# The embedding gate of an encoder layer as seven block products instead of eight, on the sums of h that the FFN needs anyway

## The chip, the cores and the metric

The kernel runs on one core of a Trainium2 chip, written in Bass with the Tile framework. Tile inserts the waits; on an engine that the code has not put under "manual schedule" it also chooses the order of the instructions, and on the others they stand as the code issues them. Each engine runs its own list in order, and an instruction that waits holds up all that stand behind it on that engine. The metric is the device time of one execution in microseconds (us). A profile of one execution goes with it, with the start and length of each instruction.

## The reference

One layer of a bidirectional encoder, 1024 tokens by 1024 features in float32. What matters here comes after the attention:

```python
h   = layer_norm(ALPHA * x + mix, ln1)                   # mix = heads @ w_out
g   = h @ w_ffn_gate ;  up = h @ w_ffn_up                # 1024 x 2816 each
ffn = (silu(g) * up) @ w_ffn_down
ple      = p @ w_ple_proj                                # p: 1024 x 256, the per-layer embedding
ple_gate = sigmoid(h @ w_ple_gate)                       # 1024 x 1024, the embedding gate
out = layer_norm(ALPHA * h + ffn + ple_gate * ple, ln2)
```

## The kernel before

Every float32 operand is held as two parts, `hi` (rounded, written by ScalarE's copy) and `lo` (the rest, written by VectorE's subtract): the helper `split`, lines 72 to 74. A product of 128 rows by 512 columns is three matmuls, hi·hi, hi·lo and lo·hi (`mm3`, lines 76 to 79, and `mm3c`, 824 to 828). The first of the three reads only the `hi` parts; the second reads the `lo` of the weights, the third the `lo` of the activations.

The program has these stages: the input projection with retention and attention (up to about 373 us in the profile), the output projection with the first layer norm (to 468 us), the embedding (to 586 us), the FFN's gate and up products, called G (to about 1000 us), and the down product with the second layer norm, called D.

In the output projection, tokens are handled in eight tiles of 128. Tile t's projection is taken out of PSUM by `zpart` (line 629, one half of the features at a time), normalised by `ln1_apply` (641 to 645; between its two halves GpSimd computes the reciprocal square root, line 639), turned by `to_hT` (653 to 663: eight TensorE transposes, ScalarE writes hi, VectorE lo) into the blocks `HB[i, j]`, with i the half of the features and j the half of the tokens, and scaled by ALPHA in place in its accumulator `accs[t]`.

The embedding stage is four calls of `ple(h, half, ...)` (734 to 760), one for each half of the output columns and of the tokens. A call is two parts. First the gate: 8 feature tiles by 4 token tiles by 3 matmuls, in four PSUM banks, so 96 matmuls, and 384 in all. Then four embeddings, each a small product of p's tile with `w_pe` (6 matmuls, lines 752 to 756); sigmoid on ScalarE (758), and on VectorE the product with the embedding (759) and the addition to the accumulator (760). The tile of p is split into a buffer `pt` of which there is one (line 750, tag "p", the 1), so the next tile of p can only be split when the six matmuls on the last one are over. No engine is under manual schedule in this stage, and Tile is free to put other matmuls between the embeddings.

G works with 2 by 2 blocks and seven products in place of eight (Winograd's form of Strassen's scheme). Its sums of the blocks of h, `TT[1]` to `TT[4]`, are made in this stage by VectorE and split (`t_sums`, 766 to 810), spread over the calls of `ple`. G's sums of weights are made by GpSimd (`s_sums`, 859 to 867). All engines are under manual schedule from G on.

Weights come through `unit2` (102 to 111): one DMA of 512 KB into one of two buffers "raw", then two splits. Buffers of TensorE's weights turn over too: eight in all, "w" and "u". PSUM has eight banks of 128 by 512, two with each of the tags mm, s, t, o.

Of the kernel before, what the change touches and what calls it, by code (L numbers as in the profile page):

```python
# [40 lines left out]
def layer(tc, xT, xn, w_first, w_mt, w_rv, w_out, w_pg, w_pe, pT, w_gu, w_dn,  # L41
# [627 lines left out]
    for kt in range(4):  # L669
        if kt % 2 == 0:  # L670
            wbig = ct([P, 2, 2, 2, HF], ("h2", "h3")[kt // 2], dt=F32R)
# [56 lines left out]
    def load_pg(h):  # L728
        r = []
        for k in range(4):  # L730
            r += unit2(w_pg[h, k], *((wp, "w") if k % 2 == 0 else (cpool, "u")))
        return r

    def ple(h, half, wpg, side=()):

        sl = slice(h * HF, (h + 1) * HF)
        bg = [bank(("mm", "s")[k // 2]) for k in range(4)]
        for kt in range(KT):
            hh = HB[kt // 4, half]
            for k in range(4):  # L740
                tt = slice(k * P, (k + 1) * P)
                mm3(bg[k], hh[:, 0, kt % 4, tt], hh[:, 1, kt % 4, tt], wpg[kt][:, 0, :], wpg[kt][:, 1, :],
                    kt == 0, kt == KT - 1)
            if kt % 2 and kt // 2 < len(side):
                side[kt // 2]()
        for k in range(4):
            t = 4 * half + k
            r = ct([P, 2 * P], "pr", 2)
            sp.dma_start(r, pT[t])
            pt = ct([P, 2, 2 * P], "p", 1, F32R)  # L750
            split(r, pt[:, 0, :], pt[:, 1, :])
            b2 = bank("to"[k % 2])
            for q in range(2):
                c = slice(q * P, (q + 1) * P)
                mm3(b2, pt[:, 0, c], pt[:, 1, c], wpe[:, h, 0, q * HF:(q + 1) * HF], wpe[:, h, 1, q * HF:(q + 1) * HF],
                    q == 0, q == 1)
            sg = ct([P, HF], "sg", 2)
            act.activation(sg, bg[k], AF.Sigmoid)
            dve.tensor_tensor(sg, sg, b2, ALU.mult)
            dve.tensor_tensor(accs[t][:, sl], accs[t][:, sl], sg, ALU.add)  # L760

    TT, tails = {}, []

    def t_sums():
# [3 lines left out]
        hi = lambda i, j, c: HB[i, j][:, 0, c, :].bitcast(F32)  # L770
        lo = lambda i, j, c: HB[i, j][:, 1, c, :].bitcast(F32)
        hold = {}

        def both(x, left, right, c):

            dve.tensor_tensor(x, hi(*left, c), hi(*right, c), ALU.subtract)
# [52 lines left out]

# [527 lines left out]
```

## Time and profile before

| | us |
|---|---|
| median of 3 runs | 1233.03 (1231.03 to 1233.54) |
| profiled execution, span from first to last instruction | 1230.3 |
| embedding stage in the profile, first gate matmul to last embedding matmul | 468.20 to 586.27 |
| TensorE busy / VectorE / ScalarE / GpSimd | 1210.4 / 721.4 / 474.9 / 367.4 |

The profile gives no separate time for its execution; the span stands 2.7 us under the median, the part of a run that lies outside the first and the last instruction and the spread of runs together. Times inside the profile are counted from the span's start. A group's busy time can include overlap: a 128 by 512 matmul is shown with 0.39 us, but the next one starts 0.23 us after it. In a row of a timeline, the bracket tells how long the engine had been idle before the instruction and which instruction let it go on.

### The profile page before, as it was taken

To read this page: it belongs to the slowest core of one execution; us is meant where nothing else is said; L and a number is where in the kernel's file an instruction comes from. 1 tells how busy PE (TensorE), PEld (TensorE's weight loads), DVE (VectorE), ACT (ScalarE), POOL (GpSimd) and SP (SyncE) were. 2 spreads that over 40 slices of the span, in tenths; PEclk is the share of its full clock that TensorE was granted. 3 is DMA by queue.
4 is the path that set the end of the run, shared out by engine and by line. 5 is a ranking of instruction groups with operands and counts; after the bars stand their busy time and mean duration, and the time that the engine had idled before them with its cause. 6 is when DMAs were issued, how large, how long until landed. Compare 5 with 4: busy or idle time off the path is not lost.

```text
span 1230.3 us, 16375 instructions
## 1 busy us (share of the span) xinstructions
PE 1210.4 (98%) x5987; PEld 1000.5 (81%) x5987; DVE 721.4 (59%) x1288; ACT 474.9 (39%) x890; POOL 367.4 (30%) x342
## 2 busy tenths in 40 slices
PE   9999999999999999999999999999999999999986
PEld 7888888888888888877888888888888888888874
DVE  5542566666755585883755554455554466773766
ACT  5643124344665024432333323233333325552562
POOL 2000011111010020000774665655646341133241
PEclk9999999999999999999999999999999999999997
DMA  6310010101004313132333222332223169999956
GB/s 253 94 35 1 18 35 19 35 19 35 18 24 161 103 52 103 34 105 111 116 128 129 77 77 103 129 129 78 92 87 129 69 216 327 355 248 222 274 111 190
DMA packets 56689, 139.64 MB, mean 114 GB/s; under 512 B 6816, under 2 KB 8992, under 8 KB 56608
## 3 DMA queue, kind: packets, MB, share of 16 engines
q1 hardware_dynamic: 47968, 121.81, 28.3%
q0 software_dynamic: 8640, 16.78, 7.8%
q8 instruction: 47, 0.77, 0.3%
q14 instruction: 34, 0.28, 0.1%
HBM read 104.75 MB, written 28.57 MB: 108 GB/s over the span
## 4 chain that ended last, share of the span: by engine, by line
PE 91%; DVE 4%; issue 1%; ACT 1%; POOL 1%; DMA 1%; DVEq 0%; SPq 0%; ACTq 0%; POOLq 0%
PE bmm L77 7%; PE bmm L78 7%; PE bmm L79 7%; PE bmm L826 4%; PE bmm L827 4%; PE bmm L828 4%; PE bs L826 4%; PE bs L827 4%; PE bs L828 4%; PE bo L827 4%; PE bo L826 4%; PE bo L828 4%; PE bt L826 4%; PE bt L828 4%; PE bt L827 4%; PE bs L79 2%
## 5 line engine op out<-in xcount | busy, mean ns | idle before, releaser
L77 PE MATMUL bmm<-H,w 128*128 128x512 f32 x240 | 100.7, 419 | 1.1 <-DVE rkq L218 0.9
L79 PE MATMUL bmm<-H,w 128*128 128x512 f32 x240 | 94.4, 393 | 0.0
L78 PE MATMUL bmm<-H,w 128*128 128x512 f32 x240 | 94.1, 392 | 0.0
L74 DVE TENSOR_TENSOR w<-raw,w 128x512 fp32r<-128x512 f32 x80 | 60.3, 763 | 52.6 <-ACT w L73 52.3
L863 POOL TENSOR_TENSOR H<-ln 128x512 f32<-128x512 f32 x22 | 28.4, 1292 | 192.3 <-PE bo L79 111.5
L893 POOL TENSOR_TENSOR ev<-ev 128x512 f32<-128x512 f32 x33 | 54.9, 1664 | 91.4 <-DVE ev L908 38.6
L481 POOL COPY sc<-skb 128x1 f32<-128x1 f32 x64 | 17.8, 288 | 202.7 <-PE bt L502 154.2
L74 DVE TENSOR_TENSOR w<-H,w 128x512 fp32r<-128x512 f32 x44 | 40.6, 924 | 63.9 <-ACT w L73 63.9
L73 ACT ACTIVATE w<-raw 128x512 fp32r<-128x512 f32 x80 | 48.9, 624 | 60.8 <-PE bmm L79 29.6
L897 POOL TENSOR_TENSOR ev<-ev,ev 128x512 f32<-128x512 f32 x44 | 62.7, 1437 | 2.6
L891 ACT ACTIVATE ev<-ev 128x512 f32<-128x512 f32 x33 | 20.9, 633 | 102.3 <-DVE ev L908 102.3
L74 DVE TENSOR_TENSOR u<-H,u 128x512 fp32r<-128x512 f32 x47 | 36.1, 767 | 40.1 <-ACT u L73 39.7
L490 ACT ACTIVATE sc<-sc,st 128x385 f32<-128x385 f32 (+1 forms) x64 | 37.2, 583 | 46.2 <-DVE st L488 46.1
L77 PEld LDWEIGHTS bmm<-H,w 128*128 128x128 f32 x240 | 45.3, 189 | 11.4 <-DVE rkq L218 2.2
L486 DVE CUSTOM_DVE_ANT_0 sc<-cst,bs,skb 128x384 f32<-128x384 f32 (+1 forms) x64 | 35.0, 574 | 32.6 <-PE bs L485 32.6
L79 PEld LDWEIGHTS bmm<-H,w 128*128 128x128 f32 x240 | 45.0, 188 | 10.1
L78 PEld LDWEIGHTS bmm<-H,w 128*128 128x128 f32 x240 | 45.3, 189 | 6.1
L73 ACT ACTIVATE u<-H 128x512 fp32r<-128x512 f32 x47 | 29.6, 631 | 43.1 <-PE bs L828 14.0
L639 POOL TENSOR_TENSOR stt<-stt,cst 128x1 f32<-128x1 f32 x8 | 11.6, 1454 | 99.6 <-DVE stt L638 99.6
L867 POOL TENSOR_TENSOR H<-raw,H 128x512 f32<-128x512 f32 x22 | 37.8, 1717 | 0.0
L448 POOL TENSOR_TENSOR sm<-sm,cst 128x8 f32<-128x8 f32 x8 | 13.9, 1737 | 78.4 <-DVE sm L447 78.4
L73 ACT ACTIVATE w<-H 128x512 fp32r<-128x512 f32 x44 | 27.4, 622 | 24.4 <-PE bs L828 6.3
(644 smaller groups left out, 3719.7 us busy)
## 6 DMA issues: line engine op xcount, KB each, us to landing
ad<-ev SPq DMA_DIRECT2D x33, 512.0 KB, 2.6
raw<-in_w_gu SPq DMA_DIRECT2D x22, 512.0 KB, 4.3
ln<-in_w_gu SPq DMA_DIRECT2D x22, 512.0 KB, 3.5
raw<-ad SPq DMA_DIRECT2D x40, 256.0 KB, 5.8
ln<-ad SPq DMA_DIRECT2D x37, 256.0 KB, 6.4
H<-in_w_dn SPq DMA_DIRECT2D x33, 256.0 KB, 6.8
raw<-in_w_mt SPq DMA_DIRECT2D x14, 512.0 KB, 3.5
h0b<-in_w_dn POOLq DMA_DIRECT2D x24, 256.0 KB, 7.0
```

The source lines that it names most:

```text
L73: act.activation(hi, raw, AF.Copy)
L74: dve.tensor_tensor(lo, raw, hi.bitcast(F32), ALU.subtract)
L77: pe.matmul(o, lh, rh, start=start, stop=False)
L78: pe.matmul(o, lh, rl, start=False, stop=False)
L79: pe.matmul(o, ll, rh, start=False, stop=stop)
L490: act.activation(sc[g][:, :nk + 1], sc[g][:, :nk + 1], AF.Exp, bias=st_[:, 1, j, g:g + 1], accum_out=st_[:, 2, j, g:g + 1])
L826: pe.matmul(o, lh, rh, start=start, stop=False, skip_group_check=True)
L827: pe.matmul(o, lh, rl, start=False, stop=False, skip_group_check=True)
L828: pe.matmul(o, ll, rh, start=False, stop=stop, skip_group_check=True)
L867: pool.tensor_tensor(s[3], a(0, 1), s[0], ALU.subtract)
L893: pool.tensor_tensor(c[:, 1, :], c[:, 0, :], c[:, 1, :], ALU.mult)
L897: pool.tensor_tensor(self.ev[dst][:, 0, :], left, right, op)
```

## The change

The gate `h @ w_ple_gate` is computed in G's form: seven block products `prod(p, ...)` of 48 matmuls each, 336 in all, on `HB` and the same sums `TT`. With it goes:

- The sums of blocks of the gate's weights (products 5, 6, 7 and 3) are made in DRAM. SP issues four DRAM-to-DRAM copies of 1 MB (`wsum_copy`), GpSimd's queue seven DRAM-to-DRAM accumulating DMAs of 1 MB (`wsum_add`), both in the code of the retention stage. SP's and GpSimd's lists are not under manual schedule there.
- The halves of the tokens change places in G and D (`HB` in other buffers, `RIGHT`, `tile_of`), since the sum `TT[3]` is now made from the first half alone, at the stage's start: three VectorE operations of 128 by 1024 on one half of it, three GpSimd operations on the other. `TT[2]`, `TT[1]`, `TT[4]` follow one by one with two VectorE operations for each half.
- VectorE combines the seven products out of PSUM into tiles `u`, `v`, `f` (128 by 512): 24 operations in all, 8 of them between product 1 and product 2, since product 2 adds into the banks that product 1 wrote.
- `accs[t]`, scaled, is stored to DRAM (`zd`) right behind its transposes; gate times embedding is added to it there, by 16 accumulating DMAs of 256 KB on GpSimd's queue (`embed`), in place of 16 VectorE additions.
- TensorE is put under manual schedule in the whole stage. Eight embeddings stand in two groups of four with nothing between them; the eight others in `embed_last`, two before and two after the first unit of G, and G's first weight sums stand behind them.

The core of the diff:

```diff
+    wblk = lambda h, i: w_pg[h, 2 * i:2 * i + 2]
+    wsum = {5: (ws[0], [(1, 0), (1, 1)]), 6: (ws[1], [(1, 0), (1, 1), (0, 0)]),
+            7: (ws[2], [(1, 0), (0, 0)]), 3: (ws[3], [(1, 0), (1, 1), (0, 0), (0, 1)])}
+    def wsum_copy():
+        for t, parts in wsum.values():
+            sp.dma_start(t, wblk(*parts[0]))
+    def wsum_add(n):
+        for t, parts in wsum.values():
+            if n < len(parts):
+                pool.dma_start(t, wblk(*parts[n]), accum_op=ALU.add, max_dma_last_dim=4096)
...
+        wsum_copy()
         for i in range(1, NPAIR):
+            wsum_add(i)
...
         act.activation(accs[t], accs[t], AF.Copy, scale=ALPHA)
+        sp.dma_start(zd[t], accs[t])
...
+    def t3():
+        TT[3] = big16((P, 2, 4, HF))
+        for q, e in enumerate((dve, pool)):
+            x, c = xs3[q], qs_[q]
+            e.tensor_tensor(x, hi(0, 0, c), hi(1, 0, c), ALU.subtract)
+            e.tensor_tensor(x, x, lo(0, 0, c), ALU.add)
+            e.tensor_tensor(x, x, lo(1, 0, c), ALU.subtract)
+        for q in range(2):
+            put(3, xs3[q], qs_[q])
...
+    def prod(p, bs, start, stop, side=()):
+        w, L = pg(p, nprod[0]), LEFT[p]()
+        nprod[0] += 1
+        for kt in range(4):
+            for k in range(4):
+                c = slice(k * P, (k + 1) * P)
+                mm3c(bs[k], L[:, 0, kt, c], L[:, 1, kt, c], w[kt][:, 0, :], w[kt][:, 1, :],
+                     start and kt == 0, stop and kt == 3)
+            if kt < len(side):
+                side[kt]()
...
+    def embed(t, h, pt, b2, f):
+        for q in range(2):
+            c = slice(q * P, (q + 1) * P)
+            mm3(b2, pt[:, 0, c], pt[:, 1, c], wpe[:, h, 0, q * HF:(q + 1) * HF], wpe[:, h, 1, q * HF:(q + 1) * HF],
+                q == 0, q == 1)
+        dve.tensor_tensor(f, f, b2, ALU.mult)
+        pool.dma_start(zd[t][:, h * HF:(h + 1) * HF], f, accum_op=ALU.add)
...
+    with tc.manual_schedule(engines={mybir.EngineType.PE}):
+        t3()
+        bs = banks(MS)
+        prod(3, bs, True, True, [lambda: to_hT(4), lambda: None, lambda: to_hT(5)])
...
+        prod(7, bs, True, True, [lambda: to_hT(6), lambda: None, lambda: to_hT(7)])
...
+        prod(1, bs, True, False)
+        for k in range(4):
+            dve.tensor_tensor(u[k], u[k], bs[k], ALU.subtract)
+            dve.tensor_tensor(v[k], v[k], bs[k], ALU.add)
+        t2(0)
+        t2(1)
+        prod(2, bs, False, True)
...
+        for k in range(4):
+            embed(4 + k, 0, ptile(4 + k), b2[k], f[k])
...
+        prod(6, by, True, False)
...
+        prod(4, bs, True, True)
...
+        prod(5, by, False, True)
+        for k in range(4):
+            dve.tensor_tensor(v[k], v[k], by[k], ALU.subtract)
+            act.activation(v[k], v[k], AF.Sigmoid)
+            dve.tensor_tensor(u[k], u[k], by[k], ALU.add)
+            act.activation(u[k], u[k], AF.Sigmoid)
+        b2 = banks(MS)
+        for k in range(4):
+            embed(4 + k, 1, ptile(4 + k), b2[k], f[k])
+    def embed_last(k):
+        pt = ptile(k)
+        for h, f in enumerate((v[k], u[k])):
+            embed(k, h, pt, bank("to"[h]), f)
...
     with tc.manual_schedule(engines={ET.PE, ET.DVE, ET.Activation, ET.Pool, ET.SP}):
+        embed_last(0)
+        ahead(2, 2)
+        embed_last(1)
         ahead(2, 4)
         for k in range(NG):
             gunits[k][1]()
+            if k == 0:
+                embed_last(2)
+                embed_last(3)
+                for part in range(2):
+                    for m in range(2):
+                        pairs2[0].s_sums(m, (part,))
             gunits[k][2]()
```

Three places in the lists of the engines. In these rows the letters name the tile (the number is its buffer's), and the line is that of the kernel listed: `split`'s lo is L74 before and L78 in the change, `zpart` L629 and L648, the two halves of `ln1_apply` L644, L645 and L663, L664.

The first place is VectorE's list at the start of the gate, where the last token tile leaves the output projection. Before, from `zpart` on the tile's first half (w_4130 to w_4149 are the gate's weights, acc_4005 is the tile):

```order
L629 SCALAR_TENSOR_TENSOR acc_4005<-sg_4077,bmm_4007 128x512
L74 TENSOR_TENSOR w_4130<-raw_4128,w_4130 128x512
L633 BN_STATS stt_4006<-acc_4005 128x6
L629 SCALAR_TENSOR_TENSOR acc_4005<-sg_4078,bs_4008 128x512
L74 TENSOR_TENSOR w_4133<-raw_4128,w_4133 128x512
```

In the change, from the second half of the same tile (now acc_4027); ahead of these rows stand w_4160, w_4163, `zpart` on the first half and L775, the first of the three operations on f_4139. H_4143 is `TT[3]`, f_4139 and f_4140 its two halves before the split, and w_4168 is the third of the four weight tiles of product 3:

```order
L648 SCALAR_TENSOR_TENSOR acc_4027<-sg_4101,bs_4030 128x512
L776 TENSOR_TENSOR f_4139<-f_4139,h_3782 128x1024
L652 BN_STATS stt_4028<-acc_4027 128x6
L777 TENSOR_TENSOR f_4139<-f_4139,h_3783 128x1024
L656 BN_AGGR stt_4028<-stt_4028 128x2
L78 TENSOR_TENSOR H_4143<-f_4140,H_4143 128x1024
L657 TENSOR_SCALAR stt_4028<-stt_4028 128x1
L663 SCALAR_TENSOR_TENSOR acc_4027<-acc_4027,stt_4028,ln_3741 128x1024
L78 TENSOR_TENSOR H_4143<-f_4139,H_4143 128x1024
L664 SCALAR_TENSOR_TENSOR acc_4027<-acc_4027,stt_4028,ln_3743 128x1024
L78 TENSOR_TENSOR w_4168<-raw_4166,w_4168 128x512
```

The third weight tile stood directly behind the first `zpart` before; it stands behind the three sums, both splits of `TT[3]` and both halves of the layer norm now. The other half of the sum is on GpSimd, ahead of the last tile's reciprocal square root (L658):

```order
L658 TENSOR_TENSOR stt_3947<-stt_3947,cst 128x1
L775 TENSOR_TENSOR f_4140<-h_3782,h_3783 128x1024
L776 TENSOR_TENSOR f_4140<-f_4140,h_3782 128x1024
L777 TENSOR_TENSOR f_4140<-f_4140,h_3783 128x1024
L658 TENSOR_TENSOR stt_4028<-stt_4028,cst 128x1
```

Before, GpSimd had only the row of L639 (now L658) for each tile here.

The second place is TensorE's list where one embedding follows another. Before (p_4314 and p_4330 are two tiles of p in the one buffer, h_4105 is a block of h in the next gate product):

```order
L79 MATMUL bt_4317<-H_4111,p_4314 128x512
L77 MATMUL bmm_4379<-w_4122,h_4105 128x512
L78 MATMUL bmm_4379<-w_4122,h_4105 128x512
L79 MATMUL bmm_4379<-w_4122,h_4105 128x512
L77 MATMUL bo_4333<-H_4111,p_4330 128x512
L78 MATMUL bo_4333<-H_4111,p_4330 128x512
L77 MATMUL bmm_4380<-w_4122,h_4105 128x512
L79 MATMUL bo_4333<-H_4111,p_4330 128x512
```

In the change, from the last matmul on one tile of p to the third on the next (mm3 is now lines 81 to 83):

```order
L83 MATMUL bmm_4521<-H_4130,p_4527 128x512
L81 MATMUL bmm_4522<-H_4130,p_4540 128x512
L82 MATMUL bmm_4522<-H_4130,p_4540 128x512
L83 MATMUL bmm_4522<-H_4130,p_4540 128x512
L81 MATMUL bmm_4522<-H_4130,p_4540 128x512
```

Four matmuls of the gate stood between them before, and none stands there now.

The third place is VectorE's list behind the last product. Before, an embedding's rows were product, split of the next tile of p, addition (sg_4324 is the gate, bt_4317 the embedding in PSUM):

```order
L759 TENSOR_TENSOR sg_4324<-sg_4324,bt_4317 128x512
L74 TENSOR_TENSOR p_4330<-pr_4328,p_4330 128x256
L760 TENSOR_TENSOR acc_3726<-acc_3726,sg_4324 128x512
L776 TENSOR_TENSOR ln_4407<-h_4106,h_4105 128x1024
L759 TENSOR_TENSOR sg_4340<-sg_4340,bo_4333 128x512
```

In the change (f_4254 and f_4255 are v, f_4360 and f_4361 are u, bt_4588 to bo_4591 product 5's banks; two more rows like the first stand ahead):

```order
L887 TENSOR_TENSOR f_4254<-f_4254,bt_4589 128x512
L889 TENSOR_TENSOR f_4360<-f_4360,bt_4589 128x512
L887 TENSOR_TENSOR f_4255<-f_4255,bo_4590 128x512
L889 TENSOR_TENSOR f_4361<-f_4361,bo_4590 128x512
L887 TENSOR_TENSOR f_4255<-f_4255,bo_4591 128x512
L889 TENSOR_TENSOR f_4361<-f_4361,bo_4591 128x512
L842 TENSOR_TENSOR f_4656<-f_4656,bmm_4827 128x512
L78 TENSOR_TENSOR p_4846<-pr_4844,p_4846 128x256
L842 TENSOR_TENSOR f_4656<-f_4656,bmm_4828 128x512
L78 TENSOR_TENSOR p_4859<-pr_4857,p_4859 128x256
```

The product with the embedding still stands ahead of the next split of p, and eight operations on product 5's banks now stand ahead of the group's first.

SP's list has the four copies (L564) between the loads of `w_rv` early in the program, at about 20 to 50 us of the profile before; GpSimd's list has the first three accumulating DMAs ahead of the fills of the score tiles (L481 before).

More of the change, by code (lines that the diff above doesn't have):

```diff
@@ L50, in layer @@
     ps = ent(tc.tile_pool(name="ps", bufs=2, space=PSUM))
+    dr = ent(tc.tile_pool(name="dr", bufs=1, space=bass.MemoryType.DRAM))
+    zd = dr.tile([NT, P, D], F32, name="zd")
+    ad = dr.tile([NHID // 2, 4, P, 2, HF], F32, name="ad")
+    ws = [dr.tile([2, P, D], F32, name=f"ws{k}") for k in range(4)]
     cstack = ent(contextlib.ExitStack())
@@ L670, in layer @@
         if kt % 2 == 0:
[L671 removed]
+            wbig = ct([P, 2, 2, 2, HF], ("h0a", "h0b")[kt // 2], dt=F32R)
         r = rawt(2 * HF)
@@ L726, in layer @@
         split(r, wpe[:, h, 0, :], wpe[:, h, 1, :])
[L728 to L760, printed above, removed]
@@ L812, in layer, with pg @@
[L812 to L822 removed]
+    def pg(p, k):
+        src = wsum[p][0] if p in wsum else wblk(*{1: (0, 0), 2: (0, 1), 4: (1, 1)}[p])
+        ts = []
+        for q in range(2):
+            ts += unit2(src[q], *((wp, "w") if k % 2 == 0 else (cpool, "u")))
+        return ts
@@ L828, in mm3c, with atile, put @@
         pe.matmul(o, ll, rh, start=False, stop=stop, skip_group_check=True)
-    RIGHT = {1: HB[0, 0], 2: HB[1, 0], 3: HB[1, 1], 4: TT[4], 5: TT[1], 6: TT[2], 7: TT[3]}
+    TT = {}
+    hi = lambda i, j, c: HB[i, j][:, 0, c, :].bitcast(F32)
+    lo = lambda i, j, c: HB[i, j][:, 1, c, :].bitcast(F32)
+    qs_ = [slice(2 * q, 2 * q + 2) for q in range(2)]
+    def atile():
+        return big.tile([P, 2, HF], F32, tag="A", bufs=8, name=nm("f"))
+    def put(n, x, c):
+        split(x, TT[n][:, 0, c, :], TT[n][:, 1, c, :])
@@ new lines, in layer, with less @@
+    xs3 = [atile() for _ in range(2)]
+    def t3():
[7 more added lines that the diff above has]
+            put(3, xs3[q], qs_[q])
+    def less(x, i, j, c, y):
+        dve.tensor_tensor(x, hi(i, j, c), y, ALU.subtract)
+        dve.tensor_tensor(x, x, lo(i, j, c), ALU.add)
@@ new lines, in banks, with quad, ptile @@
+    def banks(tags):
+        return [bank(t) for t in tags]
+    def quad():
+        ts = [atile() for _ in range(2)]
+        return [ts[k // 2][:, k % 2, :] for k in range(4)]
+    def ptile(t):
+        r = ct([P, 2 * P], "pr", 2)
+        sp.dma_start(r, pT[t])
+        pt = ct([P, 2, 2 * P], "p", 1, F32R)
+        split(r, pt[:, 0, :], pt[:, 1, :])
+        return pt
+    def embed(t, h, pt, b2, f):
+        for q in range(2):
+            c = slice(q * P, (q + 1) * P)
[3 more added lines that the diff above has]
+        pool.dma_start(zd[t][:, h * HF:(h + 1) * HF], f, accum_op=ALU.add)
@@ L1175, in dpost @@
                     later.append([steps[j - i][i] for i in range(3) if 0 <= j - i < 4])
-                later.append([lambda u=u: sp.dma_start(out[u], accd[u]) for u in range(4, NT)])
+                later.append([lambda u=u: sp.dma_start(out[tile_of(u)], accd[u]) for u in range(4, NT)])
         elif p == 7:
```

112 lines of the change are left out of this document (52 added, 60 removed).

## The prediction

> **What bounds the kernel now.** I read the page's busy shares and chain of waits first, then the stretches of the program, then the timelines of the engines in the stage that is changed.
>
> ```profile
> PE 1210.4 (98%) x5987; PEld 1000.5 (81%) x5987; DVE 721.4 (59%) x1288; ACT 474.9 (39%) x890; POOL 367.4 (30%) x342
> PE 91%; DVE 4%; issue 1%; ACT 1%; POOL 1%; DMA 1%; DVEq 0%; SPq 0%; ACTq 0%; POOLq 0%
> 468.20:586.30 118.10, 117.94 (x526) 94.57 (x525) 77.54 (x108) 44.17 (x71) 1.52 (x1) 1.00 0.26 86
> 586.30:1000.00 413.70, 413.70 (x1827) 342.66 (x1826) 218.70 (x277) 131.20 (x221) 237.31 (x160) 1.00 0.30 108
> ```
>
> The last two rows are stretches of the span: their length, then busy time and instructions of TensorE (PE), its weight loads, VectorE (DVE), ScalarE (ACT) and GpSimd (POOL), the granted clock, the DMA share and GB/s. TensorE is on 91% of the chain, and in the changed stage, the third row, it is busy for 117.94 of 118.10 us at the full clock (1.00). So a matmul taken out there is worth its pitch, and a wait put in there costs its whole length. The pitch comes from 36 matmuls without a gap at the start of G:
>
> ```profile
> 586.27 0.40 PE L826 MATMUL bmm<-h0a,u 128*128 128x512 f32 x1
> 594.45 0.39 PE L826 MATMUL bs<-H,w 128*128 128x512 f32 x1
> ```
>
> 8.18 us over 36 is 0.227 us. The transposes of one token tile are two groups of four:
>
> ```profile
> 450.07 0.60 PE L660 MATMUL bt<-cst,acc 128*128 128x128 f32 x4
> 450.50 0.60 PE L660 MATMUL bo<-cst,acc 128*128 128x128 f32 x4
> ```
>
> 0.43 us a group, 0.87 for a tile.
>
> **What is removed.** The gate has 336 matmuls instead of 384: 48 x 0.227 = 10.9 us. The stage before lasts from 468.20 to 586.27, 118.1 us. Packed, its 480 matmuls, the 12 of G that run inside it and the transposes of four token tiles (3.5 us) would take 492 x 0.227 + 3.5 = 115.2, so it loses 2.9 us now in small gaps. The same work in the change, packed, is 444 x 0.227 + 3.5 = 104.3 us. **If TensorE's waits in the new stage sum to S, the time changes by S - 13.8 us.** The rest is S, at five places.
>
> **1. The start of product 3.** VectorE's list decides when its third weight tile, w_4168, is there.
>
> ```profile
> 468.20 0.39 PE L77 MATMUL bmm<-w,h0a 128*128 128x512 f32 x1
> 469.20 0.50 PE L77 MATMUL bmm<-w,h0a 128*128 128x512 f32 x1 [0.16 <-DVE acc L629]
> 464.62 0.68 DVE L662 TENSOR_TENSOR h0b<-bo,h0b 128x512 fp32r<-128x512 f32 x1
> 467.25 1.29 DVE L74 TENSOR_TENSOR w<-raw,w 128x512 fp32r<-128x512 f32 x2 [1.96 <-ACT w L73]
> 468.47 0.68 DVE L629 SCALAR_TENSOR_TENSOR acc<-sg,bmm 128x512 f32<-128x512 f32 x1
> 469.11 0.69 DVE L74 TENSOR_TENSOR w<-raw,w 128x512 fp32r<-128x512 f32 x1
> 473.42 1.27 DVE L644 SCALAR_TENSOR_TENSOR acc<-acc,stt,ln 128x1024 f32<-128x1024 f32 x1
> 474.62 0.68 DVE L74 TENSOR_TENSOR w<-raw,w 128x512 fp32r<-128x512 f32 x1
> ...
> 497.39 1.22 DVE L776 TENSOR_TENSOR ln<-h,h 128x1024 f32<-128x1024 f32 x1
> 498.53 0.68 DVE L759 TENSOR_TENSOR sg<-sg,bo 128x512 f32<-128x512 f32 x1
> ```
>
> From one start to the next, an operation of 128 by 512 takes 0.6 us, a sum of 128 by 1024 1.14, half a layer norm 1.20. Up to 468.47 the list is the old one. Then, as the order stands: two `zpart` and two statistics (4 x 0.6), three sums (3.42), both splits of `TT[3]` (2.28), the layer norm's two halves (2.4), small ones (0.3), w_4168 (0.6): 11.4 us, so it is written at 479.9. TensorE starts the gate at 468.20 and wants it after 24 matmuls, one `to_hT` (0.87), one more matmul and the 0.3 us that its second bank is late today (469.20), at 475.1. The wait is at least **4.8 us**. The layer norm there waits on nothing else, but the split of f_4140 waits on GpSimd (POOL), whose three sums can begin when the last h of the first half is out of PSUM:
>
> ```profile
> 462.97 0.59 ACT L661 ACTIVATE h0b<-bo 128x512 fp32r<-128x512 f32 x1
> 234.29 0.67 POOL L354 TENSOR_TENSOR sq<-sq,masks 128x256 f32<-128x256 f32 x1
> 606.26 1.29 POOL L864 TENSOR_TENSOR H<-H,raw 128x512 f32<-128x512 f32 x1
> 606.79 1.31 DVE L74 TENSOR_TENSOR u<-raw,u 128x512 fp32r<-128x512 f32 x1 [1.95 <-ACT u L73]
> ```
>
> No GpSimd operation of 128 by 1024 is in this trace. From 0.67 us for 256 elements and 1.29 for 512 I estimate 2.53. From 463.56 the three end at 471.2 at the earliest, before VectorE asks. But the last two rows show what they do to VectorE meanwhile: its split, 0.68 us alone, started 0.53 us into a GpSimd operation and ended at 608.10, 0.55 after that one's end. It stood still. A VectorE operation with both inputs in SBUF then waits a whole GpSimd operation, here 2.5 us. The splits of w_4160 and w_4163 (467.25 to 468.47 now) fall into the three: the first ends 0.55 after the second sum, at 469.7, and if GpSimd gets in between, the other after the third, at 472.8. All that stands behind is 4.3 us later, and the wait is **9.1 us**. I take 7.4, nearer the upper end, since the row shows the blocking and only the turns are unknown.
>
> The Trainium skill states this as a rule against such a change (SBUF — State Buffer, "Who interferes with whom"): VectorE with two SBUF inputs and a GpSimd operation that reads SBUF exclude each other for a whole instruction. By that rule the sum has 9.1 here and the time is 1.7 us above my forecast; with both running side by side 4.8, and 2.6 below it. The row at 606.79 agrees with it.
>
> **2. Between products 1 and 2.** Each of four banks takes two VectorE operations before product 2 may add to it.
>
> ```profile
> L759 DVE TENSOR_TENSOR sg<-sg,bt 128x512 f32<-128x512 f32 x8 | 5.5, 685 | 17.0 <-PE bt L79 17.0
> ```
>
> At 0.6 us apart, this kind out of PSUM, the eight take 4.8. TensorE comes back to the last bank 18 matmuls (4.1 us) after it left the first: a wait of 0.9 if VectorE is free. It isn't: behind the last token's transposes stand 10.3 us of sums and splits (eight of 1.14, two of 0.6), from about the start of product 1, whose first bank is ready 8.9 us on. That makes it up to 3.1. I take 2.3.
>
> **3. Embedding behind embedding.** This chain is in today's trace, filled with other matmuls:
>
> ```profile
> 551.00 0.39 PE L79 MATMUL bt<-H,p 128*128 128x512 f32 x1
> 551.23 0.39 PE L77 MATMUL bmm<-w,h0a 128*128 128x512 f32 x1
> 551.95 0.50 PE L77 MATMUL bo<-H,p 128*128 128x512 f32 x1
> 552.28 0.39 PE L78 MATMUL bo<-H,p 128*128 128x512 f32 x1
> 552.75 0.39 PE L79 MATMUL bo<-H,p 128*128 128x512 f32 x1
> 551.48 0.42 ACT L73 ACTIVATE p<-pr 128x256 fp32r<-128x256 f32 x1 [2.17 <-PE bt L79]
> 551.50 0.69 DVE L759 TENSOR_TENSOR sg<-sg,bt 128x512 f32<-128x512 f32 x1 [3.98 <-PE bt L79]
> 552.10 0.42 DVE L74 TENSOR_TENSOR p<-pr,p 128x256 fp32r<-128x256 f32 x1
> ```
>
> The last matmul on one p tile starts at 551.00; ScalarE's hi begins at its end, VectorE's product comes first, then its lo; the third matmul on the next tile starts at 552.75. That is 1.75 us for 3 matmuls, 0.68: 1.07 us of waiting, today covered by four gate matmuls. In the change that cover is gone at nine borders: three in each group of four, then ahead of the first, the second and the fourth `embed_last` (12 matmuls of G cover the third). **9 x 1.07 = 9.6 us**, the firmest term. Two are dearer by the order. At the second group's first, eight operations on product 5's banks stand ahead: started on the first bank, they end 2.9 us behind the product, then 0.6 and 0.42: 3.9 instead of the 1.8 at which the third matmul is due, 1.1 more than the 1.07. At the second `embed_last`, two products and two weight splits: 2.4 instead of 0.45, 0.9 more. I take 11.6, and up to 13 where the loads of p, queued on SP behind four of G's weights, are late too.
>
> **4. The start of G.** GpSimd's first weight sums wait, now as before, for the last embedding, and now for two more DMA issues ahead of them.
>
> ```profile
> 586.57 1.29 POOL L863 TENSOR_TENSOR H<-ln 128x512 f32<-128x512 f32 x1 [111.47 <-PE bo L79]
> 1024.92 0.88 POOL L1013 DMA_DIRECT2D h0b<-in_w_dn  x1 [0.70 <-DVE h L74]
> ```
>
> The last product (0.6) and an issue (0.88) make them 1.4 us later against TensorE. The first sum is two operations (2.9), and ScalarE's split of it (0.6) stands ahead of its copy (0.6) of the second bank, which TensorE wants 24 matmuls, 5.4 us, after the last embedding: it comes at about 5.9, so 0.5 (0 to 1.5).
>
> **5. What I cost at nothing.** The weight sums in DRAM are wanted at 467, two stages after they are issued. The stores of `zd` are spread over a queue that is idle for three quarters of the stage (0.26 above). GpSimd's accumulating DMAs of the embedding are wanted in D, 400 us on. The 16 VectorE additions that go (0.6 each) lay under TensorE, as do the new ones outside the places above. `wsum_copy` may touch the loads of `w_rv`; that is a rival.
>
> **The sum.** S = 7.4 + 2.3 + 11.6 + 0.5 = 21.8; 21.8 - 13.8 = **+8.0 us**. The profiled span goes from 1230.3 to 1238.3. I add the same to the median, 1233.03, which lies 2.7 us above the span: **1241.0 us, slower by 0.65%**. With every lower end S is 4.8 + 0.9 + 9.6 = 15.3 and the time 1234.5; with every upper end 9.1 + 3.1 + 13 + 1.5 = 26.7 and 1245.9. This case's own range is 1235 to 1246.
>
> **The rivals.**
>
> *The copies hold up the start, slower still.* Each is 1 MB in SP's queue ahead of two loads of `w_rv`.
>
> ```profile
> q0 software_dynamic: 8640, 16.78, 7.8%
> 32.77 0.33 SPq L315 DMA_DIRECT2D raw<-in_w_rv  x1
> 57.06 0.63 ACT L73 ACTIVATE qq<-raw 128x512 fp32r<-128x512 f32 x1 [2.31 <-DMA raw<-in_w_rv]
> 68.38 0.60 ACT L333 ACTIVATE rv<-bmm 128x512 f32<-128x512 f32 x1 [0.80 <-PE bmm L79]
> ```
>
> No DRAM-to-DRAM transfer is in the trace. Accumulating ones into SBUF moved 16.78 MB in 7.8% of 1230.3 us, 96 us, so 1 MB takes 6. The last load of `w_rv` is split at 57.06 and wanted at about 67.5, by the last matmuls behind the row at 68.38: 10 us to spare. Three copies lie in the way of that load. At 6 us each they fill gaps that the queue has anyway; from some 8.5 us each TensorE waits, three times what is over. At 10 us: 4.5 more, 1245.5. Chance 0.12.
>
> *The waits are there at their lower ends, no change that can be told.* VectorE and GpSimd do not meet at product 3, and VectorE is free at product 2: 1234.5, in the 0.2% around 1233.03 (1230.6 to 1235.5), about what a measurement of this kernel can tell from none. The row at 606.79 speaks against it. Chance 0.12.
>
> *Faster.* VectorE makes `TT[3]`'s sums before the last tile comes: h of the first half is complete at 465.3 (the row at 464.62), and VectorE is idle for 1.96 us before 467.25. Then w_4168 is not late, product 2 finds VectorE ahead, and S is the nine borders and 0.9: 10.5, below the 13.8 from which the change pays: 1229.7. Against it stands the order: the sums are listed behind the tile's first `zpart`, which cannot run before 468.47. Chance 0.09.
>
> **The numbers.** The forecast has 0.67. Slower by over 0.2%: it and the first rival, 0.79. Within 0.2%: 0.12. Faster: 0.09. The range of eight in ten leaves out the faster case and the upper part of the first rival: 1231.5 to 1250.
>
> **What would show it.** Right: 48 fewer matmuls; TensorE idle 5 to 9 us in front of w_4168's product, released by VectorE's split; about 1 us in front of each embedding inside a group, released by p's split; VectorE's splits beside GpSimd's three sums ending half a microsecond behind one of them. Wrong: w_4168 split before 476, embeddings 0.23 us apart, or TensorE waiting in the stretch 40 to 70 us for `rv`.

## The result and the profile after

The changed kernel takes 1277.85 us (median of 4 runs, 1275.32 to 1279.82), the one before 1233.28 (4 runs, 1231.03 to 1235.92): a ratio of **1.0363 [1.0349, 1.0377]**, slower by 44.6 us. The forecast was 1241.0 with a range up to 1250: the sign was right, the size wrong by a factor of more than five.

The page of the changed kernel, busy times and chain of waits:

```profile
PE 1220.6 (96%) x5939; PEld 1000.7 (78%) x5939; DVE 733.7 (57%) x1299; ACT 483.2 (38%) x906; POOL 394.1 (31%) x368
PE 80%; DVE 7%; issue 5%; DMA 3%; ACT 3%; POOL 2%; DVEq 0%; SPq 0%; POOLq 0%; ACTq 0%
```

TensorE has 48 matmuls fewer (5987 to 5939), and yet it is shown busy for 10 us longer: many of those left run at a lower clock (0.978 on average, 0.995 before). Its share of the chain falls from 91 to 80%. To see where the 47.7 us of the span (1230.3 to 1278.0, the profile being of the slowest of the four runs) come from, the same instruction is looked up in both kernels. GpSimd's power in the last retention step, before and then after:

```profile
362.24 1.64 POOL L448 TENSOR_TENSOR sm<-sm,cst 128x8 f32<-128x8 f32 x1 [13.18 <-DVE sm L447]
```

```profile
387.75 1.64 POOL L452 TENSOR_TENSOR sm<-sm,cst 128x8 f32<-128x8 f32 x1 [13.18 <-DVE sm L451]
635.31 1.61 POOL L927 TENSOR_TENSOR H<-ln 128x512 f32<-128x512 f32 x1
```

The second row of after is GpSimd's first weight sum of G, at 586.57 before. So **25.5 us are lost by the end of the attention, and 23.2 more in the gate**; one comes back later. The prediction had 0 and 8.0.

**The attention.** A stretch near its start, as a window (columns as in the prediction's), before and after:

```profile
62.00:80.00 18.00, 17.97 (x103) 14.55 (x102) 9.18 (x29) 8.40 (x21) 1.31 (x4) 1.00 0.19 60
```

```profile
62.00:80.00 18.00, 12.28 (x35) 7.35 (x33) 5.48 (x10) 5.94 (x14) 1.25 (x3) 0.65 0.73 217
```

35 instructions of TensorE in place of 103, at a clock of 0.65. The chain of waits in this stretch of after (start, length, what) names what it waits for:

```profile
65.02 2.51 DMA raw<-in_w_rv
68.94 4.87 DMA raw<-in_w_rv
75.21 8.19 DMA raw<-in_w_rv
```

SP's issues and ScalarE's first split of `w_rv`, before and then after:

```profile
28.57 26.25 SPq L315 DMA_DIRECT2D raw<-in_w_rv  x8
31.21 0.63 ACT L73 ACTIVATE A<-raw 128x512 fp32r<-128x512 f32 x1
```

```profile
30.59 11.21 SPq L319 DMA_DIRECT2D raw<-in_w_rv  x2
65.02 0.93 SPq L319 DMA_DIRECT2D raw<-in_w_rv  x2
66.00 0.49 SPq L564 DMA_DIRECT2D ws<-in_w_pg  x1
62.12 0.60 ACT L494 ACTIVATE sc<-sc,st 128x385 f32<-128x385 f32 x1
62.72 1.14 ACT L77 ACTIVATE A<-raw 128x512 fp32r<-128x512 f32 x2
```

Before, eight loads followed one another from 28.57 and the first was split at 31.21. After, the first two loads went out between 30.59 and 41.80, but **the first split stands in ScalarE's list behind the softmax exponentials of the first two attention steps (62.12)** and runs at 62.72. There are two raw buffers; while the split stands back neither comes free, and the third load isn't issued before 65.02. By then every load meets copies and accumulating DMAs. Most of the loss is made here: GpSimd's power in the first retention step is already 22.9 us late. The other 2.6 us come up around 196 us, where TensorE waits 2.26 us for VectorE and then runs at half clock; that place was not looked into. The issues, median us to landing in the last column, before and after:

```profile
raw<-in_w_rv SPq DMA_DIRECT2D x8, 256.0 KB, 2.5
```

```profile
raw<-in_w_rv SPq DMA_DIRECT2D x8, 256.0 KB, 5.0
ws<-in_w_pg SPq DMA_DIRECT2D x4, 7.3
ws<-in_w_pg POOLq DMA_DIRECT2D x7, 1024.0 KB, 8.3
```

**The gate.** TensorE waits at every place the prediction named, and at one it had nearly free. Rows of its timeline, after (brackets: idle before, releaser):

```profile
495.02 0.50 PE L755 MATMUL bmm<-w,h 128*128 128x512 f32 x1 [0.85 <-DVE w L78]
498.39 0.80 PE L754 MATMUL bmm<-w,h 128*128 128x512 f32 x1 [2.63 <-DVE acc L648]
510.00 0.50 PE L755 MATMUL bmm<-w,h 128*128 128x512 f32 x1 [2.67 <-DVE w L78]
556.71 0.50 PE L81 MATMUL bmm<-H,p 128*128 128x512 f32 x1 [0.78 <-ACT p L77]
562.47 0.50 PE L81 MATMUL bs<-H,p 128*128 128x512 f32 x1 [1.68 <-ACT p L77]
619.54 0.79 PE L81 MATMUL bt<-H,p 128*128 128x512 f32 x1 [8.31 <-ACT p L77]
```

The windows behind the second and the third row, in front of the last and behind it:

```profile
498.30:504.00 5.70, 5.61 (x18) 4.65 (x18) 5.70 (x9) 2.03 (x3) 0.00 (x0) 0.50 0.27 92
511.20:514.40 3.20, 3.20 (x10) 2.42 (x9) 1.75 (x3) 0.05 (x1) 0.00 (x0) 0.50 0.76 200
609.00:619.50 10.50, 2.23 (x10) 1.50 (x8) 2.67 (x4) 1.69 (x4) 1.72 (x2) 0.71 0.97 252
619.60:623.60 4.00, 4.00 (x10) 3.13 (x11) 1.03 (x2) 0.93 (x2) 0.00 (x1) 0.50 0.10 34
```

The first, the second and the last show something no term of the sum has: behind these waits TensorE runs at **half clock** (0.50, a matmul every 0.43 us instead of 0.227), for 5.7, 3.2 and 4.0 us. The third is the stretch of the 8.3 us wait for a tile of p: the DMAs are 97% busy. SP's rows there:

```profile
603.29 0.46 SPq L919 DMA_DIRECT2D raw<-in_w_gu  x1
603.80 0.42 SPq L919 DMA_DIRECT2D ln<-in_w_gu  x1
604.27 0.43 SPq L919 DMA_DIRECT2D raw<-in_w_gu  x1
604.75 0.97 SPq L919 DMA_DIRECT2D ln<-in_w_gu  x1
605.81 14.49 SPq L831 DMA_DIRECT2D pr<-in_pT  x3
```

Four loads of 512 KB stand ahead of p's next tile, with the accumulating DMAs of `zd` beside them. The tile's load, issued at 605.81, takes 13.2 us to land; the median of p's loads is 4.7.

From TensorE's timeline between 493.8 and 635 each matmul's start, less the start before it and the pitch, gives what is lost; where a releaser is named or the gap is over 0.5 us it is counted as a wait, else as slower matmuls:

| step of the prediction | predicted | waits | slower matmuls |
|---|---|---|---|
| 1. start of product 3 | 7.4 | 6.6 | 4.9 |
| 2. between products 1 and 2 | 2.3 | 1.3 | 0.5 |
| 3. embeddings, without the next row | 11.6 | 10.1 | 3.9 |
| 3. second `embed_last`: load of p | in 11.6 | 8.5 | |
| 4. start of G, and the rest | 0.5 | 0.5 | 0.5 |
| S | 21.8 | 27.0 | 9.8 |

36.8 in all; the break-even of 13.8 and the lag's 23.2 ask for 37.0. Of the 9.8, some 6.5 us are the half clock: 12.9 us of matmuls at twice their pitch in the three windows with 0.50. The rest comes at a clock of 1.00, where the matmul behind the first one after a wait follows some 0.1 us late (0.34 us in place of 0.227 behind 556.71).

### The profile page after: what moved, and what is told of

Same layout as the page of the kernel before. It is cut to its first block, busy times and chain, and to the rows that moved or that the text cites. A ratio compares the mean times of both kernels' runs of the same rounds, so it can differ in the third digit from the quotient of the medians.

```text
span 1278.0 us, 16371 instructions
## 1 busy us (share of the span) xinstructions
PE 1220.6 (96%) x5939; PEld 1000.7 (78%) x5939; DVE 733.7 (57%) x1299; ACT 483.2 (38%) x906; POOL 394.1 (31%) x368
## 4 chain that ended last, share of the span: by engine, by line
PE 80%; DVE 7%; issue 5%; DMA 3%; ACT 3%; POOL 2%; DVEq 0%; SPq 0%; POOLq 0%; ACTq 0%
PE bmm L81 5%; PE bmm L83 5%; PE bmm L82 5%; PE bo L754 4%; PE bs L754 4%; PE bo L756 4%; PE bo L755 4%; PE bt L756 4%; PE bt L755 4%; PE bt L754 4%; PE bs L756 4%; PE bs L755 4%; PE bmm L754 4%; PE bmm L755 4%; PE bmm L756 4%
## 5 line engine op out<-in xcount | busy, mean ns | idle before, releaser
L78 DVE TENSOR_TENSOR w<-raw,w 128x512 fp32r<-128x512 f32 x92 | 73.0, 808 | 71.2 <-ACT w L77 70.9
L77 ACT ACTIVATE w<-raw 128x512 fp32r<-128x512 f32 x92 | 56.2, 627 | 86.0 <-PE bmm L83 29.3
L78 DVE TENSOR_TENSOR w<-H,w 128x512 fp32r<-128x512 f32 x44 | 42.1, 957 | 66.4 <-ACT w L77 66.4
L78 DVE TENSOR_TENSOR u<-H,u 128x512 fp32r<-128x512 f32 x47 | 37.0, 787 | 39.3 <-ACT u L77 38.8
L843 POOL DMA_DIRECT2D zd<-f x16 | 14.0, 874 | 115.2 <-DVE f L842 73.4
L658 POOL TENSOR_TENSOR stt<-stt,cst 128x1 f32<-128x1 f32 x8 | 11.6, 1454 | 94.3 <-DVE stt L657 94.3
L508 ACT ACTIVATE ptr<-bt 128x384 f32<-128x384 f32 (+1 forms) x64 | 26.1, 456 | 33.2 <-PE bt L506 33.2
```

The costliest lines, as they stand in the source:

```text
L77: act.activation(hi, raw, AF.Copy)
L78: dve.tensor_tensor(lo, raw, hi.bitcast(F32), ALU.subtract)
```

## The experiments

All ratios are to the kernel before, run on the same chip.

**The copies by themselves.** Two readings of the 25.5 us stand against each other: the transfers hold up the loads, or the order of the lists does, which Tile chooses anew once the copies are in the program. `b_copies` is the kernel before with the four copies and seven accumulating DMAs and nothing else (their sums are read by nobody); `b_copies_order` has in addition ScalarE's and VectorE's lists held in the old order up to the first attention steps; `b_lateorder` has no DMA added, and only the first split of `w_rv` moved to where the change has it.

```diff
+        wsum_copy()                       # b_copies, b_copies_order
         for i in range(1, NPAIR):
+            wsum_add(i)
```

```diff
+    for names, order in zip(done, (OLD_ACT, OLD_DVE)):     # b_copies_order
+        for x, y in zip(order, order[1:]):
+            tc.add_manual_dep(names[y], names[x].name, NoSync)
```

```diff
+                if i == 0 and n == 1 and g == 1:           # b_lateorder: e is the second step's last exponential
+                    behind(rvs[0], e.ins.name)
```

> The kernel before with the four DRAM copies and the seven accumulating DMAs added and nothing else changed; what they write is never read. Theory A (the 25.5 us by which the changed kernel is behind at the end of attention come from these DMAs alone): 1258 us, within 2 of it. Rival (they come from the new gate, through the order that the planner chose for the whole program): 1233 to 1238.

> The same DMAs in the kernel before, but ScalarE's and VectorE's lists held in the order they had before up to the first attention steps, so that the splits of w_rv again stand ahead of the first softmax. What the DMAs write is never read. Theory A1 (the order does the harm: the splits free the two raw buffers too late): 1233 to 1240. Rival A2 (the 11 MB on the queues do it, whatever the order): 1253 to 1260. Rival A3 (GpSimd's list does it, where accumulating DMAs wait for copies ahead of the sinks' copies): the waits of GpSimd stay, 1245 to 1258.

> The kernel before without any of the DMAs, but with the first split of w_rv held behind the first two softmax steps, as the planner put it in the changed kernel. Theory A1 in its pure form (the order alone): about 8 us, 1241, since the eight loads then go through two buffers from 63 us on at 2 us each, and TensorE wants the last at 67.5. If order and copies only do harm together: 1235 to 1243, far from 1258. Rival A2: no change, 1233.

Measured: `b_copies` 1256.65, 1.0194 [1.0172, 1.0217]; `b_copies_order` 1252.47, 1.0157 [1.0133, 1.0181]; `b_lateorder` 1242.68, 1.0072 [1.0056, 1.0089]. So the DMAs alone make nearly the whole loss of the attention (23 us of 25.5), with no gate in it, and they move the order too (the first split of `w_rv` runs at 63.28 in `b_copies`); the order alone, without one added byte, makes 9:

```profile
60.00:80.00 20.00, 15.62 (x55) 10.00 (x53) 7.69 (x16) 8.89 (x18) 0.37 (x2) 0.83 0.37 115
```

But the old order does not save it as long as the copies stand ahead of the loads: ScalarE's list then blocks on splits whose loads are late, and TensorE waits earlier (40 to 62 us):

```profile
40.00:62.00 22.00, 12.66 (x49) 9.99 (x48) 8.90 (x14) 9.92 (x19) 3.40 (x4) 0.79 0.78 190
```

Neither reading is enough alone; they do not add up, since they delay the same matmuls.

**The copies elsewhere.** The changed kernel with SP's copies behind a load of `w_mt` issued at 176 us, and the accumulating DMAs after them (`a_held`); the same with these chained behind the last copy of the sinks (`sc<-skb`) on GpSimd's list and the first layer norm's power behind them (`a_held2`).

```diff
-            sp.dma_start(t, wblk(*parts[0]))
+            behind(sp.dma_start(t, wblk(*parts[0])), loads[-1])
...
-        wsum_copy()
         for i in range(1, NPAIR):
-            wsum_add(i)
+            if i == 2:
+                wsum_copy()
+            if i > 1:
+                wsum_add(i - 1)
```

> The changed kernel with the copies held behind the seventh of the later loads of w_mt, and the accumulating DMAs after them; nothing else. ScalarE's list up to there is again the old one. Theory A1 or A2: the early loss goes, 1277.9 - 25.5 = 1252.4, within 2. Rival (the copies cost the same wherever they are, by the traffic they make): 1265 or more.

> The changed kernel with the copies held as in a_held and all seven accumulating DMAs held behind the last attention's sink copies, one behind the other, product 3's block first; GpSimd's first layer-norm power behind them. Theory G (while one 1 MB accumulating DMA runs, GpSimd cannot issue the next for some 8 us, and the sinks' copies of the attention stand behind it in its list): the loss before the gate goes, 1277.9 - 25.5 = 1252.4, within 2.5. Rival T (the accumulating traffic itself slows the stage it runs in, or product 3 now waits for its block): 1258 or more.

Measured: `a_held` 1278.59, 1.0355 [1.0322, 1.0388]; `a_held2` 1274.78, 1.0347 [1.0332, 1.0363]. No gain to speak of, for two different reasons. In `a_held` the copies cost nothing any more, and GpSimd's burst took the loss over. Its windows, and GpSimd's rows:

```profile
200.00:250.00 50.00, 49.65 (x349) 42.12 (x349) 31.76 (x84) 19.50 (x49) 8.89 (x16) 1.00 0.03 12
250.00:300.00 50.00, 30.36 (x185) 25.37 (x185) 19.68 (x60) 13.57 (x34) 8.94 (x15) 0.76 0.72 129
```

```profile
252.67 1.15 POOL L575 DMA_DIRECT2D ws<-in_w_pg  x1 [0.38 <-issue]
261.45 0.91 POOL L575 DMA_DIRECT2D ws<-in_w_pg  x1 [7.63 <-issue]
270.62 0.89 POOL L575 DMA_DIRECT2D ws<-in_w_pg  x1 [8.25 <-issue]
279.28 0.90 POOL L575 DMA_DIRECT2D ws<-in_w_pg  x1 [7.78 <-issue]
287.93 0.88 POOL L575 DMA_DIRECT2D ws<-in_w_pg  x1 [7.75 <-issue]
288.49 0.85 POOL L491 COPY sc<-skb 128x1 f32<-128x1 f32 x4
```

**One accumulating DMA of 1 MB keeps GpSimd from issuing the next for about 8 us**, though these have different destinations. The small copies of the sinks, which the softmax needs, stand in the same list behind five of them; once the last is issued they run at once (288.49). In `a_held2` the attention is nearly free of it (the power of the last retention step at 365.37, 3.1 late), but now Tile has put layer norms behind splits of weights in the output projection, and TensorE has 11.39 of 20 us between 460 and 480. It waits for the second half of a layer norm, in front of which VectorE does splits of weights that land only at 479.6 and 481.7:

```profile
485.05 1.11 PE L692 MATMUL bt<-cst,acc 128*128 128x128 f32 x4 [13.65 <-DVE acc L677]
```

The loss has moved once more.

Then the accumulating DMAs one at a time, each between two sinks copies of the last two attentions (236 to 350 us), the copies at 67 us (`a_spread`), and that with the lists of ScalarE, VectorE and GpSimd held in the old kernel's order for the whole attention (`f_order`):

```diff
+            if i >= 2 and todo and n % 2:                   # a_spread: one accumulating DMA
+                wsum_add(*todo.pop(0))
```

```diff
+    for names, order in zip(emitted, (OLD_ACT, OLD_DVE, OLD_POOL)):   # f_order
+        for x, y in zip(order, order[1:]):
+            tc.add_manual_dep(names[y], names[x].name, NoSync)
```

> The changed kernel with the copies held behind the second of the later loads of w_mt and the seven accumulating DMAs put singly between the sinks' copies of the last two attentions, every second step; the lists of the gate are those of the changed kernel, row for row. Theory G (GpSimd cannot issue an accumulating DMA while one runs; alone between other work it costs nothing): the loss in attention goes and none comes in its place, 1277.9 - 25.5 = 1252.4, within 2.5. Rival T (the traffic itself costs): 1260 or more.

> a_spread (copies behind the second later load of w_mt, the seven accumulating DMAs singly between sinks' copies) with ScalarE's, VectorE's and GpSimd's lists of the whole attention held in the order that they have in the kernel before. a_spread still lost 13 us in attention. Theory O (the rest of the loss is the order that the planner writes when it counts these DMAs): the loss goes, 1264.7 - 13 = 1252, within 3, and the gate's 23 us above stay. Rival T (it is the transfers, each held-up step next to one of the seven): within 3 of 1264.7.

Measured: `a_spread` 1264.67, 1.0269 [1.0246, 1.0291]; `f_order` 1253.49, 1.0157 [1.0142, 1.0172]. The power stands at 375.31 and 363.69, 13.1 and 1.5 us late. Same DMAs, same gate, 11.6 us apart by the order of three lists alone. In `f_order` the four copies run at 67 us and TensorE does not notice them:

```profile
62.00:80.00 18.00, 17.96 (x103) 14.58 (x102) 9.59 (x32) 8.88 (x22) 1.33 (x4) 1.00 0.91 317
```

DMAs busy for 91% there, and no wait. What is left in `f_order`, 19.3 us, is nearly all the gate.

**The gate's terms.** First on `a_held2`: `t3()` issued after product 3 (`a_t3`); p's split buffer as a ring of three (`a_p3`); both, and the embeddings set between the matmuls of products 6 and 5 and of G's first units (`a_best`).

```diff
-        pt = ct([P, 2, 2 * P], "p", 1, F32R)                # a_p3, s_p3, f_p3
+        pt = ct([P, 2, 2 * P], "p", 1, F32R) if len(np_) % 3 == 1 else ct([P, 2, 2 * P], "sg", 2, F32R)
```

> a_held2 with the sums of TT[3] emitted behind product 3 instead of ahead of it. The prediction's step 1 (they stand ahead of the third weight tile on VectorE): the waits of 6.6 us in product 3 and the 4.9 us that the lower granted clock costs after them go at least half, 3 to 10 us below a_held2. Rival (VectorE's list is full there whatever comes first): within 2 us of a_held2.

> a_held2 with a ring of three p tiles (two in the space of sg) instead of one. The prediction's step 3 (one p buffer): eight of the nine borders lose most of their 1 us, 6 to 9 us below a_held2, while the 8.5 us in front of the second embed_last, which waits for a load of p, stay. Rival (the borders wait for VectorE and the loads, not for the buffer): within 3 us of a_held2.

> a_held2 with T3's sums behind product 3, the p ring, and every embedding put between other matmuls: those of the second token half between the quarters of products 6 and 5, the last four between the first units of G. If the waits of the gate are what the trace says (27.0 us of waits and 9.8 us of lower clock), S falls from 36.8 to some 5 to 8: 1252.4 - 30 = 1222, range 1219 to 1230, faster than the kernel before. Rival (new waits take their place: G's weights or the sums of GpSimd come late, the same total): 1240 to 1250.

Measured: 1275.73, 1.0361 [1.0341, 1.038]; 1260.84, 1.0237 [1.0219, 1.0254]; 1267.08, 1.0282 [1.0259, 1.0305]. The ring is worth 14 us. Moving `t3()` alone does nothing that can be told, and both together with covered embeddings lose 6 of the ring's 14 again; why, was not settled.

The same on `a_spread`: the ring (`s_p3`); `t3()` inside product 3 (`s_t3`); both, with the splits of `w_pe` behind product 7 and the loads of p ahead of G's weights (`s_all`).

```diff
-        t3()
-        prod(3, bs, True, True, [lambda: to_hT(4), lambda: None, lambda: to_hT(5)])
+        prod(3, bs, True, True, [lambda: to_hT(4), t3, lambda: to_hT(5)])     # s_t3, s_all
```

> a_spread with a ring of three p tiles. Theory from a_p3 (the one p buffer makes nearly all of the border waits, and part of the wait for the load in front of embed_last): 12 to 16 us below a_spread. The prediction's step 3 (borders of 1.07): 6 to 9.

> a_spread with the sums of TT[3] emitted after the first quarter of product 3, so that VectorE's list has all four weight tiles of product 3 ahead of them. The prediction's step 1: the waits in product 3 (6.6 us) and the lower clock behind them (4.9) go for the most part, 6 to 11 us below a_spread. Rival (product 7 waits for TT[3] instead): within 3.

> a_spread with both, the splits of w_pe put behind product 7, and the p loads of embed_last ahead of G's weights. If the waits are additive S falls from 36.8 to 5 to 12: 1233.3 - 13.8 + S = 1224 to 1232, at or below the kernel before. Rival (G's weights come late in exchange): 1236 to 1242.

Measured: 1250.9, 1.0151 [1.0131, 1.017]; 1261.0, 1.024 [1.0218, 1.0263]; 1251.92, 1.0157 [1.014, 1.0173]. The ring is worth 13.8 again. `t3()` inside product 3 takes 3.7 off by itself, where 6 to 11 were expected; in the profiles the way from GpSimd's power to G's first weight sum is 5.7 us shorter, and the attention ahead of it 1.9 longer. With the ring and the two other moves it adds nothing (`s_all`). GpSimd still made half of `TT[3]` in `s_all`.

**Both halves together.** On `f_order`: the ring (`f_p3`); then `TT[3]` wholly on VectorE and inside product 3, the splits of `w_pe` behind product 7, three buffers for p's loads, p's last tiles loaded ahead of their embeddings, and G's first two pairs of weights ahead of the second group of embeddings (`f_all2`); that with half of `TT[3]` back on GpSimd (`f_all2_pool`); and with the last four accumulating DMAs of `zd` behind GpSimd's first eight sums for G (`f_all3`).

```diff
-        for q, e in enumerate((dve, pool)):                 # f_all2, f_all3
+        for q, e in enumerate((dve, dve)):
...
-        pool.dma_start(zd[t][:, h * HF:(h + 1) * HF], f, accum_op=ALU.add)    # f_all3
+        add = lambda: pool.dma_start(zd[t][:, h * HF:(h + 1) * HF], f, accum_op=ALU.add)
+        add() if t not in (2, 3) else adds.append(add)
```

> f_order with a ring of three p tiles. As s_p3 against a_spread: 12 to 15 us below f_order, 1237 to 1241 if theory O holds.

> f_p3 with all sums of TT[3] on VectorE and emitted inside product 3, the splits of w_pe behind product 7, three buffers for the loads of p, and the first two of G's weight pairs loaded ahead of the second group of embeddings. S falls to some 6 to 10 and the attention loses nothing: 1233 - 13.8 + 8 = 1227, range 1224 to 1232, faster than the kernel before. Rival (waits move to G's weights or to VectorE at product 7): 1234 to 1242.

> f_all2 with one half of TT[3]'s sums back on GpSimd. The prediction's step 1 (VectorE with two inputs in SBUF stands still while a GpSimd operation on SBUF runs): three GpSimd sums of 2.4 to 3.3 us hold VectorE up longer than the three sums of 1.14 that it is spared, so 2 to 6 us slower than f_all2. Rival (GpSimd takes half of the work off VectorE): 0 to 3 us faster.

> f_all2 with the last four accumulating DMAs of the embedding issued behind GpSimd's first eight sums of G's weights instead of ahead of them. In f_all2 TensorE waits 3.8 us at the start of G, and GpSimd's first sum starts 5 us after the last embedding matmul, behind these issues. Theory: 2 to 4 us faster than f_all2, 1224 to 1226. Rival (GpSimd's sums wait for the last embedding anyway): within 1 us of it.

Measured: `f_p3` 1240.16, 1.0044 [1.0028, 1.0061]; `f_all2` **1227.6, 0.9945 [0.9929, 0.9962]**; `f_all2_pool` 1232.81, 1.0005 [0.9991, 1.0019]; `f_all3` **1226.32, 0.9953 [0.9937, 0.997]**. The wait that stood at 619.54, in `f_order` and then in `f_p3`:

```profile
594.07 0.79 PE L141 MATMUL bt<-H,p 128*128 128x512 f32 x1 [9.06 <-ACT p L137]
```

```profile
582.08 0.50 PE L141 MATMUL bt<-H,p 128*128 128x512 f32 x1 [2.57 <-ACT p L137]
```

In `f_p3` only two short waits of the kind are left beside it, 0.28 and 0.67 us for tiles of the ring; in `f_all2` one of 0.21. So the ring takes out more than the borders. SP issues G's four loads behind a load of p that waits for a buffer, from 578.19 on in `f_order`; with the ring that buffer comes free earlier, and they go out while the products still run:

```profile
550.37 0.42 SPq L1003 DMA_DIRECT2D raw<-in_w_gu  x1
```

`f_all2` changes several things at once, and only one of them was tried by itself: `f_all2_pool` tells what GpSimd's half of the sum costs. VectorE's rows there and GpSimd's beside them, then VectorE's of `f_all2`:

```profile
465.66 7.10 DVE L138 TENSOR_TENSOR w<-raw,w 128x512 fp32r<-128x512 f32 x3 [0.46 <-ACT w L137]
466.73 2.73 POOL L859 TENSOR_TENSOR f<-f,h 128x1024 f32<-128x1024 f32 x1
469.54 2.67 POOL L860 TENSOR_TENSOR f<-f,h 128x1024 f32<-128x1024 f32 x1
```

```profile
465.43 1.29 DVE L138 TENSOR_TENSOR w<-raw,w 128x512 fp32r<-128x512 f32 x2 [0.47 <-ACT w L137]
467.96 0.69 DVE L138 TENSOR_TENSOR w<-raw,w 128x512 fp32r<-128x512 f32 x1 [1.24 <-ACT w L137]
```

Three splits take 7.10 us beside GpSimd and end at 472.76; without it they end at 468.65. Between the two kernels lie 5.2 us (medians, measured on two chips; 7.4 by their ratios to the kernel before; G's first weight sum is 6.3 us earlier in the profile). `f_all3` removes a wait of 3.8 us at the start of G, but two others of 1.7 and 1.3 us come up 20 us on; it can't be told from `f_all2`.

So the change's idea pays 6 to 7 us, of the 10.9 that the matmuls are worth, once the DMAs, the lists and the two buffers are put right. Both versions beat the kernel before, by half a per cent.

## Why the prediction was wrong, and where it was right

**What I cost at nothing (step 5) is where 25.5 of the 39.7 microseconds are that the profile has above the forecast** (47.7 against 8.0; 15.2 are in the gate, 1.0 comes back). It put the weight sums at nothing because they are wanted late. What mattered was what they stand in front of. Its rival "the copies hold up the start" looked at the right place and gave the tell-tale, TensorE waiting in 40 to 70 us for `rv`, which came true. But it priced each copy (6 us, harmless up to 8.5; measured 7.3) against a queue that goes on as before. Three things were missing. ScalarE's list is Tile's in that stage, and had moved: the first split of `w_rv` stands behind two softmax steps (`b_lateorder`: 9 us from that alone). With two raw buffers a late split holds back every later load. And the accumulating DMAs on GpSimd's queue share the DMAs with these loads, and hold up GpSimd's list: in after it stands for 19.91 us, up to 73.44, in front of the third of them, until a copy has landed, with the copies of the sinks behind it. What that part costs by itself was not tried. The lists of the engines showed the first already; I had read them at the gate only.

**Step 3, embedding behind embedding.** The borders came out as worked out: 10.1 us of waits in place of 9.6 to 11.6, and the ring of p tiles takes 13.3 to 14 us out, these and a part of the wait for the load. What failed is its last clause, "up to 13 where the loads of p are late too". That load is 8.5 us late: four loads of 2 MB in all and the accumulating DMAs stand ahead of 128 KB, and the clause had allowed 1.4 us for it without working it out.

**The clock was in no term.** The sum charged every wait its length. After the longest waits TensorE also ran at half clock, some 6.5 us in the gate, and behind the waits it started slowly, some 3 us more: together a third on top of the waits. The Trainium skill (TensorE: Matmul & The Clock Gate, "Part 1: The HAM clock gate (the "warmup" mystery)") says the clock falls to one half after an idle window of about 3.4 us and comes back after as long a busy one; the window at 498.30 agrees on the half, but a wait of 2.63 us, with matmuls and a wait of 0.85 ahead of it, was enough, and the half clock lasted some 5.7 us. A wait of 1.68 us, in front of 562.47, did not bring the clock down.

**Right were** the break-even (that S and the lag agree to 0.2 us is bookkeeping, since both come from the same stage; it says that the pitch and the count of matmuls hold), step 1's mechanism and the size of its waits (6.6 for 7.4), and steps 2 and 4. Step 1's upper end, 9.1, was worked out 0.5 too high: two sums of 2.53 from 463.56 and 0.55 more end at 469.2, not 469.7. Step 1's blocking is seen in its clearest form in after: two splits of 0.68 us took 5.25 us beside the last two of GpSimd's three sums:

```profile
492.48 5.25 DVE L78 TENSOR_TENSOR w<-raw,w 128x512 fp32r<-128x512 f32 x2 [1.60 <-ACT w L77]
492.03 2.39 POOL L776 TENSOR_TENSOR f<-f,h 128x1024 f32<-128x1024 f32 x1
494.50 2.69 POOL L777 TENSOR_TENSOR f<-f,h 128x1024 f32<-128x1024 f32 x1
```

It was split differently: besides the 2.67 us for w_4168 (forecast 5 to 9) there is a wait of 2.63 for a bank, since the delay kept `zpart` from emptying it. GpSimd's 128 by 1024 sum takes 2.4 to 2.7 us, estimated 2.53. The Trainium skill's rule cited there (SBUF — State Buffer, "Who interferes with whom") is borne out by `f_all2` against `f_all2_pool`.

With the attention's loss gone (`f_order`), the prediction's own part of the program gives 1253.5, still 12 us above 1241.0. In after the late p and the slower matmuls are 18.3 us, and steps 1 to 3 waited 3.3 less than forecast.

## What to carry to other kernels

Where a scheduler orders some of the lists, a change in one place can reorder a stage that it never mentions: read the order of every engine there, and look for the first instruction that gives back a buffer which loads wait for. A background transfer costs little by its bytes (91% busy DMAs cost nothing where nothing waited) and much by its place: ahead of a small load that is wanted soon, or ahead of a small operation on the engine that issues it. And take what comes after a wait into its price: with the lower clock and the slow start, the waits cost a third more than their length here.

## What the runs showed of the hardware

Beside the half clock told above:

- Accumulating DMAs from DRAM to DRAM, 1 MB each, follow one another on GpSimd only every 8.7 to 9.2 us in `a_held` (7.6 to 8.3 idle, then 0.9 to issue), about the 8.5 us one takes to land there, and every 8.6 to 11.4 us in `a_held2`. Other GpSimd work runs at once behind an issue, so one at a time costs under a microsecond. The Trainium skill (DMA: Bandwidth & Descriptors, "SWDGE vs HWDGE vs iDMA") says that only one software queue is allocated for GpSimd's DMAs; that this is the cause was not tried.
- Four copies of 1 MB issued within 2.4 us took nothing from TensorE, at 176 us in `a_held` (busy for 28.98 us from 170 to 200, 29.00 before) and at 67 us in `f_order`.
